# Attention scores from operands stacked on 128 partitions, and a new order of the mixer steps, in a two-layer hybrid encoder

## The chip, the cores and the metric

The kernel runs on one core of one Trainium2 chip. The metric is the device time of one execution in microseconds (us); lower is better. The profile is of one execution on that core.

## The reference, cut to what matters

The program is an encoder of two layers over 512 tokens of 1024 features, batch 1, float32 in and out. Each layer projects the normalised input once, sends the columns through three mixers, joins them, and ends with a two-matrix feed-forward part.

```python
for i in range(DEPTH):                                   # DEPTH = 2
    h = rmsnorm(x, norm_mix_g[i])
    p = h @ w_in[i]                                      # 1024 -> 2176 columns
    a_x, a_g, q, k, v, c_u = jnp.split(p, splits, axis=-1)
    y_a = rglru_mixer(a_x, a_g, ...)                     # gated linear recurrence, both directions
    y_b = window_attention(q, k, v, attn_sink[i], ...)   # 6 query heads, 2 key heads, |i-j| <= 128
    y_c = hyena_mixer(c_u, ...)                          # long convolution through a Fourier transform
    y = concatenate([rmsnorm(y_a), rmsnorm(y_b), rmsnorm(y_c)])
    x = x + y @ w_out[i]
    x = x + square(relu(rmsnorm(x) @ w_up[i])) @ w_down[i]
return rmsnorm(x, final_norm_g)

# inside window_attention, per block of 128 queries and its neighbouring blocks of keys
s = einsum("bnqhgd,bnshd->bnhgqs", qb, kb) * 64 ** -0.5  # the scores, contraction over 64
p = exp(s - m); denom = sum(p) + exp(sink - m)
o = einsum("bnhgqs,bnshd->bnqhgd", p / denom, vb)
```

## The kernel before, in words

**Precision.** TensorE multiplies in a rounded 32-bit format (float32r). To keep float32 accuracy, an operand is split into a rounded part hi and the remainder lo (`split`, L486), and a product is made of three: hi·hi, hi·lo, lo·hi (`mm3`, L501). Weights are split as they arrive (`split_weight`, L534): ScalarE or VectorE rounds, VectorE or GpSimd subtracts.

**Stages of a layer.** First 17 input tiles (`in_tile`, L876): each is 8 x 3 products of 512 columns into the PSUM tile `pin`, and VectorE takes it out. Tiles 0 to 5 belong to the recurrence (0-2 values, 3-5 gate), 6 to 8 are the queries (each tile has one head of key head 0 on partitions 0 to 63 and one of key head 1 on 64 to 127), 9 the keys, 10 the values, 11 to 16 the convolution. Then come the mixers, which overlap the input tiles as far as the order allows; then the output projection (`po`, L1168), then the feed-forward part (`up` L1186, `down` L1215: tiles `pu`, `pX`, `pY`, `pZ`). The filters of the convolution (`filters`, L757) are computed in layer 0's mixers for layer 0, and in layer 0's feed-forward part for layer 1.

**Attention** (`attention`, L992) is a generator of 8 units per layer: 4 query blocks times 2 key heads. A unit makes three score tiles `s`, one for each query head of the group. A score tile has 256 columns in the first and last query block and 384 in the two in the middle, so 24 tiles of either kind in the two layers. Each is three products with a contraction over 64 partitions (L1014 to L1016), then one or two bfloat16 mask products over 128 partitions (L1018, L1020). VectorE takes the row maximum `mx`, ScalarE the exponential `e` with its row sum, VectorE the reciprocal `es`; the rows are scaled, transposed on TensorE (`pt`), copied out (`pth`) and multiplied by the values (`pv`).

**The order.** `SCRIPTS` (L27) is an order of the steps of each layer, written out by hand: a number is an input tile, G0 to G2 the gates of the recurrence, S its scans, A its output gate, F the filters, I two further tables and the residual input, H the convolution, R the set-up of the attention (transposed values, and the queries and keys that `in_tile` has left in `proj`), U one attention unit, NA, NB, NC the three group norms. The script gives every operation its place in a list. A planner (`Plan.schedule`, L276) then runs through a simulated time with a cost for each operation (`Plan.cost`, L236), gives each engine the ready operation that stands first in the list, and writes down the order. On the chip each engine executes its instructions in exactly that written order. Among the costs is that of the recurrence's scan (`tensor_tensor_scan`, L943), for which the formula at L263 is used: 0.07 + 512 x 0.00104 = 0.60 us.

**Fillers.** Where the planner finds TensorE without work for a while, it writes small bfloat16 products of constant data into its order (`filler`, L1273; tile `wk`, 256 columns). They are ordinary instructions of the written order, and their number is fixed when the program is built. The planner also keeps account of TensorE's activity (L374 to L385) and counts a product over 64 rows or fewer as 0.55 of a full one.

**Buffers and queues.** SBUF tiles of 128x512 come from 69 slots (`sp`, L466); PSUM has 7 banks for all tiles (`ps`, L468) and one for the fillers. All DMAs go through SyncE's queue. Weights are fetched in the order of the input tiles in the script (`wseq`, L520), two tiles ahead (`LA`). DMAs of F, I and G wait in the plan until an input tile has begun (`plan.gate`).

Of the kernel before, what the change touches and what calls it, by code (L numbers as in the profile page):

```python
# [10 lines left out]
F32 = mybir.dt.float32  # L11
# [3 lines left out]
ALU = mybir.AluOpType  # L15
# [9 lines left out]
PRODUCTS = ["P1", "P2", "P6", "P5", "P7", "P3", "P4"]  # L25
OUT_PAIRS = [(6, 7), (0, 1), (2, 3), (4, 5)]
SCRIPTS = [q.split() for q in (  # L27
    "0 10 F 9 G0 2 8 3 1 11 G1 I G2 6 7 12 16 5 15 R U 4 S U 14 13 H U U A U NC U U U NA NB",
    "15 1 16 12 13 G1 8 2 11 6 G2 0 7 14 G0 H 9 10 R U 4 U 3 U U U NC 5 S A U U U NB NA",
)]  # L30
LA = 2
RESERVE = 7
# [134 lines left out]
class Plan:  # L167
# [67 lines left out]
    @staticmethod  # L235
    def cost(eng, name, args, kw, out):  # L236
        n = 1
        for d in out.shape[1:]:
            n *= d
        if name == "tensor_reduce":  # L240
            n = kw["in_"].shape[1]
        psum = any(isinstance(v, View) and v.base.pool.psum for v in list(args) + list(kw.values()))
        if name.startswith("dma"):
            return (out.shape[0] * n * 4 / 360e3, None)
        if eng == "tensor":
            if name == "transpose":
                return (n / 1200.0, None)
            dt = kw["lhsT"].base.dtype
            if dt == F32:
                return (4 * n / 2400.0, None)  # L250
            if dt == F32R and n < 256:
                return (4 * n / 2400.0, None)
            return (n / 2400.0 + (0.0133 if dt == F32R else 0.0025), None)
        if eng == "scalar":
            c = (0.051 if psum else 0.093) + n * 0.000833
            c += 0.093 * sum(isinstance(kw.get(k), View) for k in ("bias", "scale", "accum_out"))
            return (c, _TABLE.get(kw.get("func")))
        ptr = sum(isinstance(kw.get(k), View) for k in ("scalar1", "scalar2", "scalar"))
        if eng == "vector":
            if name == "reciprocal":  # L260
                return (0.06 + n * 0.00627, None)
            fast = name in ("tensor_scalar", "tensor_copy") and not psum
            return (0.07 + n * (0.00052 if fast else 0.00104) + 0.06 * ptr, None)  # L263
        if name in ("tensor_scalar", "memset"):
            return (0.13 + 0.06 * ptr + n * 0.00105, None)
        return (0.15 + n * 0.0021, None)
# [186 lines left out]
def encoder_kernel(ctx, tc, xT, w_in, w_out, w_up, w_down, gates, fw, par, trig, rope, decay, zemb, ident_d, maskb_d, yT):  # L453
    real_nc = tc.nc
    nc = plan = Plan()
# [15 lines left out]
    def R(name):  # L471
        return sp.tile([128, T], F32R, name=name, tag="s")
# [383 lines left out]
    for i in range(DEPTH):  # L856
# [9 lines left out]
        proj = {}  # L866
# [6 lines left out]
        def last_mark():  # L873
            return max(marks.values()) if marks else len(plan.ops) - 1

        def in_tile(m):  # L876
            p = PSM("pin")
            w = weight(("in", i, m))
            marks[m] = len(plan.ops)
            mm_tile(p, w, xs, kcs=in_kcs)  # L880
            if 6 <= m < 10:
                s, q = Fs("rs"), Fs("rq")
                plan.prio = EVP
                nc.vector.stream_shuffle(s, p, shuf)
                nc.vector.tensor_tensor(out=q, in0=p, in1=ropet[0], op=ALU.mult)
                plan.prio = 0.0
                nc.any.tensor_tensor(out=s, in0=s, in1=ropet[1], op=ALU.mult)
                nc.any.tensor_tensor(out=q, in0=q, in1=s, op=ALU.add)
                proj[m] = split(q, "k" if m == 9 else "q")
                return  # L890
            o = Fs("p%d" % m)
            plan.prio = EVP
            nc.vector.tensor_tensor(out=o, in0=p, in1=rstd, op=ALU.mult)
            plan.prio = 0.0
            proj[m] = o
# [94 lines left out]
            return vs  # L990

        def attention(qs, ks, vs, yb):  # L992
            kh, kl = ks
            plan.prio = ATTP
            for qb in range(4):
                k0, k1 = max(0, qb - 1), min(4, qb + 2)
                nk = k1 - k0
                qc = slice(qb * 128, qb * 128 + 128)
                po = None
                first = True  # L1000
                outp = PMX("pv")
                for g in range(2):
                    rows = slice(64 * g, 64 * g + 64)
                    mx = smallb.tile([128, 4], F32, name="mx", tag="sb")
                    rs = smallb.tile([128, 4], F32, name="rs", tag="sb")
                    mn = smallb.tile([128, 4], F32, name="mn", tag="sb")
                    mx.parts = rs.parts = True
                    ss, pes = [], []
                    for j in range(3):
                        s = PMX("s")  # L1010
                        kc = slice(k0 * 128, k1 * 128)
                        o = s[:, :nk * 128]
                        qh, ql = qs[j][0][rows, qc], qs[j][1][rows, qc]
                        nc.tensor.matmul(out=o, lhsT=qh, rhs=kh[rows, kc], start=True, stop=False)  # L1014
                        nc.tensor.matmul(out=o, lhsT=qh, rhs=kl[rows, kc], start=False, stop=False)
                        nc.tensor.matmul(out=o, lhsT=ql, rhs=kh[rows, kc], start=False, stop=False)  # L1016
                        if qb > 0:
                            nc.tensor.matmul(out=s[:, 0:128], lhsT=identb, rhs=maskb[:, 0:128], start=False, stop=(qb == 3))  # L1018
                        if qb < 3:
                            nc.tensor.matmul(out=s[:, (nk - 1) * 128:nk * 128], lhsT=identb, rhs=maskb[:, 128:256], start=False, stop=True)  # L1020
                        nc.vector.tensor_reduce(out=mx[:, j:j + 1], in_=o, op=ALU.max, axis=AX.X)
                        ss.append(o)
                    nc.vector.scalar_tensor_tensor(out=mn[:, 0:3], in0=mx[:, 0:3], scalar=-0.125, in1=nsink[:, i, 3 * g:3 * g + 3], op0=ALU.mult, op1=ALU.min)
                    for j in range(3):
                        e = Fs("e")
                        act(e[:, :nk * 128], ss[j], AF.Exp, scale=0.125, bias=mn[:, j:j + 1], accum_out=rs[:, j:j + 1])
                        pes.append(e)
                    sk = cols(i, "sink", 3 * g, 3 * g + 3)
                    es = smallb.tile([128, 4], F32, name="es", tag="sb")
                    nc.vector.tensor_tensor(out=es[:, 0:3], in0=mn[:, 0:3], in1=sk, op=ALU.add)  # L1030
                    act(es[:, 0:3], es[:, 0:3], AF.Exp)
                    nc.vector.tensor_tensor(out=es[:, 0:3], in0=rs[:, 0:3], in1=es[:, 0:3], op=ALU.add)
                    nc.vector.reciprocal(out=es[:, 0:3], in_=es[:, 0:3])
                    for j in range(3):
                        e = pes[j][:, :nk * 128]
                        plan.either(
                            ("any", "tensor_scalar", dict(out=e, in0=e, scalar1=es[:, j:j + 1], scalar2=1.0, op0=ALU.mult, op1=ALU.mult)),
                            ("scalar", "activation", dict(out=e, in_=e, func=AF.Copy, scale=es[:, j:j + 1])),
                        )
                    for kb in range(nk):  # L1040
                        pt = PMX("pt")
                        for j in range(3):
                            nc.tensor.transpose(pt[:, j * 128:j * 128 + 128], pes[j][:, kb * 128:kb * 128 + 128], ident)
                        th = Fs("pth")
                        plan.either(
                            ("scalar", "copy", dict(out=th[:, :384], in_=pt[:, :384])),
                            ("vector", "tensor_copy", dict(out=th[:, :384], in_=pt[:, :384])),
                        )
                        nc.tensor.matmul(out=outp[:, :384], lhsT=vs[g][:, k0 + kb, :], rhs=th[:, :384],
                                         start=(g == 0 and kb == 0), stop=(g == 1 and kb == nk - 1))  # L1050
                    if g == 1:
                        for j in range(3):
                            nc.scalar.copy(out=yb[j][:, qc], in_=outp[:, j * 128:j * 128 + 128])
                    plan.prio = 0.0
                    yield True
                    plan.prio = ATTP
            plan.prio = 0.0
# [69 lines left out]
        for step in SCRIPTS[i]:  # L1127
# [22 lines left out]
            elif step == "R":  # L1150
                ks = proj.pop(9)
                vs = v_tokens()
                qs = [proj.pop(6 + j) for j in range(3)]
# [266 lines left out]
```

## Time and profile before

| | us |
|---|---|
| median of 3 runs | 1166.24 (1161.07 to 1176.31) |
| the profiled execution, its own time | 1163.03 |
| its span, first to last instruction | 1161.2 |
| busy: TensorE (PE) / its weight loads (PEld) | 1143.8 / 920.2 |
| busy: VectorE (DVE) / ScalarE (ACT) / GpSimd (POOL) | 907.7 / 591.0 / 198.2 |

Times are in us from the first instruction. PE is TensorE's products, PEld its weight loads, which run beside them; products are pipelined, so the start of one to the start of the next (the pitch) tells what a product costs, and the shown duration of one is longer than that. PEclk is the clock that the chip granted TensorE, as a share of 2.4 GHz: it has the levels 2.4 and 1.2 GHz, so a mean of 0.9 in a stretch means a fifth of it at 1.2. All instructions carry line 449, where the planner issues them, so tiles are told apart by name. `a<-b,c` reads: tile a is written from b and c.

### The profile page before, as it was taken

What the parts mean: (1) busy time and instruction counts of PE and PEld (TensorE: products, weight loads), DVE (VectorE), ACT (ScalarE), POOL (GpSimd) and SP (SyncE); (2) the same over time, 40 slices, a digit from 0 to 9 for tenths busy, and PEclk for the clock granted to TensorE, in tenths of its full rate; (3) what the DMA queues carried; (4) which work ended last, traced back from release to release, by engine and by line L of the source; (5) the groups of instructions that cost most, each with busy time, mean ns of one, the idle gap of its engine ahead of it and who ended that gap; (6) DMA issues with size and microseconds to landing.
All of it is one profiled execution on the core that took longest, in us unless ns stands there. A gap on an engine that the chain in (4) does not pass through costs nothing.

```text
span 1161.2 us, 14314 instructions
## 1 busy us (share of the span) xinstructions
PE 1143.8 (98%) x5337; PEld 920.2 (79%) x5337; DVE 907.7 (78%) x1389; ACT 591.0 (51%) x956; POOL 198.2 (17%) x125
## 2 busy tenths in 40 slices
PE   9999899999999999999999999999999999999997
PEld 6778677888888788888888877678888888888886
DVE  8999786556797886886988989574587887797796
ACT  7564655455455354344465464572664454455344
POOL 0212221000110132100331142110010110111031
PEclk9999899999999999999999998899999999999999
DMA  9612100221422513422243211002213322431412
GB/s 351 246 52 91 41 15 1 84 81 54 137 98 80 171 38 108 127 77 87 90 155 109 89 55 56 1 19 91 91 38 126 127 78 86 146 107 57 127 55 73
DMA packets 35133, 107.92 MB, mean 93 GB/s; under 512 B 4150, under 2 KB 6710, under 8 KB 35064
## 3 DMA queue, kind: packets, MB, share of 16 engines
q1 hardware_dynamic: 35064, 107.01, 27.9%
q8 instruction: 42, 0.69, 0.2%
q14 instruction: 27, 0.22, 0.1%
HBM read 104.90 MB, written 2.10 MB: 92 GB/s over the span
## 4 chain that ended last, share of the span: by engine, by line
PE 90%; DVE 7%; ACT 2%; issue 1%; POOL 0%; DVEq 0%; POOLq 0%; ACTq 0%
PE pu L449 30%; PE pY L449 15%; PE pin L449 11%; PE pZ L449 8%; PE po L449 7%; PE pX L449 4%; PE s L449 3%; PE wk L449 3%; PE pv L449 3%; DVE tg L449 2%; PE pt L449 1%; PE f L449 1%; PE xt L449 1%; PE gate L449 1%; DVE wl L449 1%
## 5 line engine op out<-in xcount | busy, mean ns | idle before, releaser
L449 ACT CAST wh<-wr 128x1024 fp32r<-128x1024 f32 x189 | 199.4, 1056 | 356.9 <-PE pu L449 133.6
L449 DVE TENSOR_TENSOR wl<-wr,wh 128x1024 fp32r<-128x1024 f32 (+1 forms) x176 | 220.3, 1254 | 158.3 <-ACT wh L449 154.2
L449 PE MATMUL pu<-xgh,wl 128*128 128x512 f32 x512 | 199.4, 390 | 0.0
L449 PE MATMUL pu<-xgh,wh 128*128 128x512 f32 x512 | 199.4, 389 | 0.0
L449 PE MATMUL pu<-xgl,wh 128*128 128x512 f32 x512 | 199.3, 389 | 0.0
L449 POOL TENSOR_TENSOR wl<-wr,wh 128x1024 fp32r<-128x1024 f32 x51 | 123.1, 2416 | 257.0 <-ACT wh L449 153.5
L449 PEld LDWEIGHTS pu<-xgh,wl 128*128 128x128 f32 x512 | 96.1, 188 | 21.4 <-issue 1.6
L449 PEld LDWEIGHTS pu<-xgl,wh 128*128 128x128 f32 x512 | 96.1, 188 | 19.8
L449 PEld LDWEIGHTS pu<-xgh,wh 128*128 128x128 f32 x512 | 96.1, 188 | 19.7
L449 PE MATMUL pin<-xgh,wh 128*128 128x512 f32 x272 | 107.5, 395 | 0.4 <-ACT e L449 0.4
L449 PE MATMUL pin<-xgl,wh 128*128 128x512 f32 x272 | 107.5, 395 | 0.0
L449 PE MATMUL pin<-xgh,wl 128*128 128x512 f32 x272 | 107.5, 395 | 0.0
L449 POOL TENSOR_TENSOR s<-s,h 128x256 f32<-128x256 f32 x12 | 8.9, 740 | 397.7 <-ACT wh L449 388.8
L449 DVE TENSOR_TENSOR wr<-wr 128x1024 f32<-128x1024 f32 x61 | 72.9, 1219 | 0.0
L449 PEld LDWEIGHTS pin<-xgl,wh 128*128 128x128 f32 x272 | 51.4, 189 | 12.8 <-DVE xgl L449 1.8
L449 PEld LDWEIGHTS pin<-xgh,wh 128*128 128x128 f32 x272 | 51.3, 188 | 12.6 <-issue 1.1
L449 PEld LDWEIGHTS pin<-xgh,wl 128*128 128x128 f32 x272 | 51.2, 188 | 11.4 <-issue 0.8
L449 PE MATMUL po<-wh,ygh 128*128 128x512 f32 x128 | 50.8, 397 | 0.0
L449 PE MATMUL po<-wh,ygl 128*128 128x512 f32 x128 | 50.0, 396 | 0.0
L449 PE MATMUL po<-wl,ygh 128*128 128x512 f32 x128 | 50.0, 390 | 0.0
L449 DVE SCALAR_TENSOR_TENSOR x<-pY,r,x 128x512 f32<-128x512 f32 x64 | 45.6, 745 | 4.9 <-PE pY L449 4.9
L449 DVE SCALAR_TENSOR_TENSOR x<-pY,nr,x 128x512 f32<-128x512 f32 x64 | 45.8, 744 | 2.3 <-PE pY L449 2.3
(321 smaller groups left out, 2413.5 us busy)
## 6 DMA issues: line engine op xcount, KB each, us to landing
wr<-in_w_up SPq DMA_DIRECT2D x64, 512.0 KB, 3.5
wr<-in_w_down SPq DMA_DIRECT2D x64, 512.0 KB, 4.2
wr<-in_w_in SPq DMA_DIRECT2D x33, 512.0 KB, 5.7
wr<-in_w_out SPq DMA_DIRECT2D x16, 512.0 KB, 3.4
x<-in_xT SPq DMA_DIRECT2D x16, 256.0 KB, 4.6
dec<-in_decay SPq DMA_DIRECT2D x8, 256.0 KB, 6.8
out_y<-fin SPq DMA_DIRECT2D x16, 128.0 KB, 1.8
gt<-in_gates SPq DMA_DIRECT2D x6, 256.0 KB, 3.8
```

Of the source, the lines that this page charges most:

```text
L449: getattr(getattr(nc, o.eng), o.name)(*[res(a) for a in o.args], **{k: res(v) for k, v in o.kw.items()})
```

## The change

The three products of a score tile become two. `stack_query` makes, for each of the two heads of a query tile, one tile with the rounded query on its own 64 partitions and the remainder on the other 64. `stack_key` makes, for each key head, one tile with the rounded key on both halves and one with the key's remainder on both halves. A product of the stacked query with the first is hi·hi + lo·hi, with the second hi·lo + lo·lo, each over 128 partitions. The planner gets a cost for the scan of 0.06 + 512 x 0.00207 = 1.12 us. The two scripts have a new order of the same steps.

```diff
@@ -25,8 +25,8 @@
 PRODUCTS = ["P1", "P2", "P6", "P5", "P7", "P3", "P4"]
 OUT_PAIRS = [(6, 7), (0, 1), (2, 3), (4, 5)]
 SCRIPTS = [q.split() for q in (
-    "0 10 F 9 G0 2 8 3 1 11 G1 I G2 6 7 12 16 5 15 R U 4 S U 14 13 H U U A U NC U U U NA NB",
-    "15 1 16 12 13 G1 8 2 11 6 G2 0 7 14 G0 H 9 10 R U 4 U 3 U U U NC 5 S A U U U NB NA",
+    "8 10 F 9 0 G0 1 3 2 G1 12 G2 7 11 6 R 16 15 I 4 U 5 S 14 U 13 H U NC U U U U U A NA NB",
+    "1 16 12 13 G1 8 0 2 14 G2 15 6 G0 11 7 10 H 9 R U U U 4 S U U U 3 U 5 NC A U NB NA",
 )]
 LA = 2
 RESERVE = 7
@@ -260,6 +260,8 @@
             if name == "reciprocal":
                 return (0.06 + n * 0.00627, None)
             fast = name in ("tensor_scalar", "tensor_copy") and not psum
+            if name == "tensor_tensor_scan":
+                return (0.06 + n * 0.00207, None)
             return (0.07 + n * (0.00052 if fast else 0.00104) + 0.06 * ptr, None)
         if name in ("tensor_scalar", "memset"):
             return (0.13 + 0.06 * ptr + n * 0.00105, None)
@@ -873,6 +875,35 @@
         def last_mark():
             return max(marks.values()) if marks else len(plan.ops) - 1
 
+        halves = (slice(0, 64), slice(64, 128))
+
+        def rounded(out, src):
+            plan.either(("scalar", "copy", dict(out=out, in_=src)), ("vector", "tensor_copy", dict(out=out, in_=src)))
+
+        def stack_query(q):
+
+            out = []
+            for g in range(2):
+                a, b = halves[g], halves[1 - g]
+                t = R("qs")
+                rounded(t[a], q[a])
+                nc.vector.tensor_tensor(out=t[b], in0=q[a], in1=t[a].bitcast(F32), op=ALU.subtract)
+                out.append(t)
+            return out
+
+        def stack_key(k):
+
+            out = []
+            for g in range(2):
+                a, b = halves[g], halves[1 - g]
+                h, l = R("kh"), R("kl")
+                rounded(h[a], k[a])
+                rounded(h[b], k[a])
+                nc.vector.tensor_tensor(out=l[a], in0=k[a], in1=h[a].bitcast(F32), op=ALU.subtract)
+                rounded(l[b], l[a].bitcast(F32))
+                out.append((h, l))
+            return out
+
         def in_tile(m):
             p = PSM("pin")
             w = weight(("in", i, m))
@@ -886,7 +917,7 @@
                 plan.prio = 0.0
                 nc.any.tensor_tensor(out=s, in0=s, in1=ropet[1], op=ALU.mult)
                 nc.any.tensor_tensor(out=q, in0=q, in1=s, op=ALU.add)
-                proj[m] = split(q, "k" if m == 9 else "q")
+                proj[m] = stack_key(q) if m == 9 else stack_query(q)
                 return
             o = Fs("p%d" % m)
             plan.prio = EVP
@@ -990,7 +1021,6 @@
             return vs
 
         def attention(qs, ks, vs, yb):
-            kh, kl = ks
             plan.prio = ATTP
             for qb in range(4):
                 k0, k1 = max(0, qb - 1), min(4, qb + 2)
@@ -1000,7 +1030,6 @@
                 first = True
                 outp = PMX("pv")
                 for g in range(2):
-                    rows = slice(64 * g, 64 * g + 64)
                     mx = smallb.tile([128, 4], F32, name="mx", tag="sb")
                     rs = smallb.tile([128, 4], F32, name="rs", tag="sb")
                     mn = smallb.tile([128, 4], F32, name="mn", tag="sb")
@@ -1010,10 +1039,8 @@
                         s = PMX("s")
                         kc = slice(k0 * 128, k1 * 128)
                         o = s[:, :nk * 128]
-                        qh, ql = qs[j][0][rows, qc], qs[j][1][rows, qc]
-                        nc.tensor.matmul(out=o, lhsT=qh, rhs=kh[rows, kc], start=True, stop=False)
-                        nc.tensor.matmul(out=o, lhsT=qh, rhs=kl[rows, kc], start=False, stop=False)
-                        nc.tensor.matmul(out=o, lhsT=ql, rhs=kh[rows, kc], start=False, stop=False)
+                        nc.tensor.matmul(out=o, lhsT=qs[j][g][:, qc], rhs=ks[g][0][:, kc], start=True, stop=False)
+                        nc.tensor.matmul(out=o, lhsT=qs[j][g][:, qc], rhs=ks[g][1][:, kc], start=False, stop=False)
                         if qb > 0:
                             nc.tensor.matmul(out=s[:, 0:128], lhsT=identb, rhs=maskb[:, 0:128], start=False, stop=(qb == 3))
                         if qb < 3:
```

## Rows read from the trace of the kernel before

**Rows 1.** Page, part 1: busy us, share and instructions of each engine.
```profile
PE 1143.8 (98%) x5337; PEld 920.2 (79%) x5337; DVE 907.7 (78%) x1389; ACT 591.0 (51%) x956; POOL 198.2 (17%) x125
```
**Rows 2.** Windows: length, busy PE, PEld, DVE, ACT, POOL, PEclk, DMA share, GB/s.
```profile
300.00:325.00 25.00, 25.00 (x112) 20.71 (x111) 16.93 (x22) 9.41 (x12) 2.37 (x1) 1.00 0.44 133
...
0.00:140.00 140.00, 134.14 (x596) 102.00 (x596) 128.26 (x227) 85.36 (x134) 25.60 (x22) 0.98 0.46 161
140.00:207.00 67.00, 66.42 (x402) 50.52 (x402) 49.44 (x102) 37.70 (x95) 14.64 (x12) 0.97 0.03 9
...
715.00:772.00 57.00, 56.56 (x276) 36.82 (x277) 37.42 (x97) 38.51 (x101) 9.71 (x13) 0.88 0.03 10
```
**Rows 3.** Windows of the fillers alone (tile wk): length, busy PE, PEclk, DMA.
```profile
140.00:207.00 67.00, 12.47 (x93) 0.97 0.03 9
...
715.00:772.00 57.00, 9.52 (x64) 0.88 0.03 10
```
**Rows 4.** Chain that ended last, by line: 100 to 215, then 680 to 780.
```profile
by line: PE s L449 13.8%; PE pv L449 12.4%; PE pin L449 10.1%; DVE tg L449 9.0%; PE po L449 8.9%; PE wk L449 7.9%; PE pt L449 5.9%; PE y L449 5.0%; DVE p L449 4.1%; DVE cv L449 2.9%; PE Xo L449 2.5%; PE Xe L449 2.5%; PE ssq L449 2.3%; DVE w
...
by line: PE s L449 21.9%; PE pv L449 15.2%; PE po L449 7.8%; PE pt L449 7.0%; PE wk L449 6.5%; DVE t L449 5.6%; DVE tg L449 5.2%; issue 5.2%; DVE yc L449 4.0%; PE ssq L449 2.7%; DVE wl L449 2.3%; DVE G L449 1.9%; DVE Gl L449 1.9%; DVE X L44
```
**Rows 5.** Timeline of PE, a 256-column score tile: start, us, instruction.
```profile
116.84 0.39 PE L449 MATMUL pin<-xgh,wl 128*128 128x512 f32 x1
117.15 0.38 PE L449 MATMUL s<-kh,qh 64*128 64x256 f32 x1
117.38 0.28 PE L449 MATMUL s<-kl,qh 64*128 64x256 f32 x1
117.50 0.28 PE L449 MATMUL s<-kh,ql 64*128 64x256 f32 x1
117.70 0.23 PE L449 MATMUL s<-maskb,identb 128*128 128x128 bf16 x1
117.86 0.39 PE L449 MATMUL s<-kh,qh 64*128 64x256 f32 x1
```
**Rows 6.** Timeline of PE, a 384-column score tile and the next one's start.
```profile
140.06 0.44 PE L449 MATMUL s<-kh,qh 64*128 64x384 f32 x1
...
140.99 0.44 PE L449 MATMUL s<-kh,qh 64*128 64x384 f32 x1
```
**Rows 7.** Timeline of PE, products over 128 partitions with 256 columns.
```profile
176.26 0.28 PE L449 MATMUL y<-trigl,Gh 128*128 128x256 f32 x1
176.38 0.28 PE L449 MATMUL y<-trigh,Gl 128*128 128x256 f32 x1
```
**Rows 8.** Tile qh: min/median/max ns of the queries' rounding and subtraction.
```profile
L449 DVE TENSOR_TENSOR ql<-rq,qh x6: 673/682/693, 52.2 to 666.9; 128x512 fp32r<-128x512 f32 x6
L449 DVE CAST qh<-rq x4: 409/412/429, 51.2 to 652.4; 128x512 fp32r<-128x512 f32 x4
L449 ACT CAST qh<-rq x2: 623/624/626, 100.5 to 666.3; 128x512 fp32r<-128x512 f32 x2
```
**Rows 9.** Window of DVE alone: length, busy us, PEclk, DMA share, GB/s.
```profile
25.00:125.00 100.00, 96.85 (x150) 0.98 0.37 129
```
**Rows 10.** Timeline of DVE in layer 1: the keys' first and last step.
```profile
688.95 0.67 DVE L449 TENSOR_TENSOR rq<-pin,ropet 128x512 f32<-128x512 f32 x1
...
709.84 0.68 DVE L449 TENSOR_TENSOR rq<-rq,rs 128x512 f32<-128x512 f32 x1
```
**Rows 11.** Groups by shape: the scan (count, busy us, mean ns).
```profile
L449 DVE TENSOR_TENSOR_SCAN tg<-a,tg 128x512 f32<-128x512 f32 x12 | 17.4, 1481 | 0.0
```
**Rows 12.** Timeline of PE: a stall in layer 0 (idle before, releaser).
```profile
123.13 1.54 PE L449 MATMUL pt<-ident,e 128*128 128x128 f32 x6 [2.85 <-POOL e L449]
```
**Rows 13.** Timelines around 170: fillers, what follows them, ACT's last rounding before it.
```profile
168.36 7.94 PE L449 MATMUL wk<-warmc 128*128 128x256 bf16 x56
176.06 0.36 PE L449 MATMUL y<-trigh,Gh 128*128 128x256 f32 x1
...
170.36 0.62 ACT L449 CAST Gh<-G 128x512 fp32r<-128x512 f32 x1 [1.79 <-DVE es L449]
```

## Prediction

> **What bounds the kernel now.** I read the page's busy times first: TensorE is busy for 98% of the span, VectorE for 78%, ScalarE for 51% [rows 1]. So I then cut the span into stages. In the feed-forward part TensorE starts 112 products of 512 columns in 25 us, 0.22 us each, at full clock and without a gap [rows 2]: nothing there changes. The two ends of the mixers, 140 to 207 in layer 0 and 715 to 772 in layer 1, look just as full (66.4 of 67 and 56.6 of 57 us busy), but 12.5 and 9.5 us of that are fillers [rows 3], and the granted clock is 0.97 and 0.88 [rows 2], so part of the stretch ran at 1.2 GHz. In these ends the input tiles are used up and TensorE has only the attention and the convolution.
>
> The chain of waits says what sets their length. In the 115 us from 100 the score tiles hold 13.8% of the chain, in the 100 us from 680 they hold 21.9%, more than any other tile [rows 4]: 15.9 + 21.9 = 37.8 us. The 48 score tiles cost about 39 us in all (below), so nearly all of their time is on the chain. Fillers are on it too (7.9% and 6.5%). That is the point of a written order: a filler is executed even if TensorE is late, so time lost against the plan isn't made up by leaving fillers out.
>
> **The score products.** A 256-column score tile takes 0.71 us, from 117.15 to 117.86 [rows 5]. The second of its products costs 0.12; the first lasts 0.23 until the next, the third 0.20, the mask product 0.16. The step from the 128-row product of the input tile to the first 64-row one is 0.31, where 512 columns cost 0.22. A 128-row product of 256 columns costs 0.12 as well [rows 7], so the number of rows itself costs nothing; it is the change between 64 and 128 rows, twice in each tile, that costs some 0.3 us. With two products of 128 rows the tile should take 2 x 0.12 and 0.06 for the mask (half of 256 columns; no row shows a mask without the change): 0.30, so 0.41 less. A 384-column tile takes 0.93, 140.06 to 140.99 [rows 6]; one product lies between 0.12 for 256 and 0.22 for 512, so 0.17, and the tile becomes 2 x 0.17 + 2 x 0.06 = 0.46, so 0.47 less. For 24 tiles of each kind: 24 x (0.41 + 0.47) = 21.1 us. Of that 7.0 us, 24 x (0.12 + 0.17), is the third product and 14.1 the changes of rows, a cost that no formula of the planner holds.
>
> How much reaches the end? At least nothing, if the row maxima and exponentials behind the scores set the pace at once; at most all 21.1. The chain shows 37.8 of 39 us of score time on it, which is near the upper end; but a faster score tile of 0.46 us comes close to what VectorE needs for its maximum, so that is late next. I take 85%: 17.9 us.
>
> The Trainium skill has a rule against this change: TensorE: Matmul & The Clock Gate, in the section on packing small matmuls, says that products over few rows run at the same time if they sit in different row groups, so two 64-row products could share the array and 128-row ones can't. By that rule three 64-row products would cost as much as one and a half full ones, and the change would add half a product per tile, 24 x 0.5 x (0.12 + 0.17) = 3.5 us by our rows. Rows 5 don't bear it out: the kernel before issues the three products of one head in a row, all on the same half, and each takes its full 0.12.
>
> **The added vector work.** Before, a layer had 4 roundings and 4 subtractions for three query tiles and the keys. After, each query tile has 2 and 2, the keys 6 and 2: 12 and 8. Both layers add 16 roundings and 8 subtractions. Half the partitions save nothing that I can count on, so I take the full tile's times: a rounding is 0.41 us on VectorE or 0.62 on ScalarE, a subtraction 0.68 [rows 8]. All on VectorE that is 16 x 0.41 + 8 x 0.68 = 12.0 us, 6 per layer; the other bound is nothing, if it all lies in gaps, and a gain is excluded since nothing is taken away. From 25 to 125 VectorE is busy for 96.9 of 100 us [rows 9], just where layer 0 makes these operands, so about 3 of its 6 us find room and 3 don't; the ends are emptier (49.4 of 67, 37.4 of 57) [rows 2], so I add 1 for layer 1. Cost: 4 us.
>
> The keys of layer 1 are worse placed: their tile is the last before R in both scripts, and in the old one their first vector step at 688.95 is followed by the last one only at 709.84 [rows 10], because VectorE has the convolution's work ahead of it. The first score waits for that. Before, a rounding came next; now two roundings, the subtraction and one more rounding stand in sequence for the second product: at 0.62 and 0.68 that is 1.2 to 2 us more for one head, and 5.1 for both (6 x 0.62 + 2 x 0.68) if they go one behind another, against nothing if input tiles cover it. I take 2 us.
>
> **The new order and the scan's cost.** What can be won: the stall at 123 (2.85 us, transposes ahead of input products waited for a scaled exponential) [rows 12]; the clock, where a mean of 0.98 over 140 us loses 2.8 us of work, 0.97 over 67 us 2.0 and 0.88 over 57 us 6.8 [rows 2]; and fillers past their use: 56 of them run from 168.36 to 176.06, while ScalarE's last rounding for the next products ended at 170.98, 5.1 us earlier [rows 13]. Together 19.6 us. They come from VectorE and TensorE being later than planned. The scan takes 1.48 us on average [rows 11]; the plan counts 0.60 and will count 1.12, so 0.52 of the 0.88 us that it misses, 59%, becomes known, and the changes of rows go altogether. Against that, any new order may have stalls of its own. Bounds: all 19.6 won, or 10 lost (two stalls like that at 123, with as much again in clock after each). I take about half: 9.5 us won.
>
> Of the moved steps, I has ten DMAs of 256 KB and moves in layer 0 from behind eight input tiles to behind thirteen. What it loads is first read after 176 (tables of y) and by the output projection; the DMA engines are at 3% from 140 to 207 [rows 2], so it costs nothing unless those 40 us of slack were used up. F stays third, and the number of weight fetches is the same. Tile 8 comes first instead of 0; both wait for the same norm of x. A moves behind the last U of layer 0; its three activations and three products, some 3.9 us at the 0.62 and 0.68 of tiles of that size [rows 8], can go into ScalarE's gaps beforehand or beside the first output products, which use group C. I count nothing, and 4 us in the range.
>
> **Sum.** The profiled execution took 1163.0 us, 1.8 more than its span and 3.2 below the median of the three runs. 1163.0 - 17.9 - 9.5 + 4 + 2 = 1141.6, so 1142 us: 1.8% below the profiled execution, 2.1% below the median.
>
> **The rivals.**
>
> *The saved time returns as waiting.* VectorE's maxima, ScalarE's exponentials and the 7 PSUM banks set the pace of the ends, and fillers fill what TensorE saves. For it: fillers are there already [rows 3]. Against: the scores lead the chain [rows 4]. Then a third of the 21.1 arrives, 7, the order gives 4 and the additions cost 6: 1158 us. Chance 0.22.
>
> *Everything falls into place.* All 21.1 us and nearly all of the 19.6 arrive, say 18, with 4 of additions: 1128 us. For it: both come from one cause, a plan that didn't know how late the engines were. Against: the order of before was also written by a planner. Chance 0.18.
>
> *The change of rows stays.* If the 0.3 us belonged to the change of data type at the bfloat16 mask, the masks would keep it, and only the third product goes: 7.0 x 0.85 = 6. Then 1163.0 - 6 - 8 + 6 = 1155. Against it: the step from input tile to score costs 0.09 extra though both are float32r [rows 5]. Chance 0.06. [...]
>
> *VectorE becomes the bound, and it gets slower.* It has 3.1 us free between 25 and 125 [rows 9]. If ScalarE takes no roundings, 12.0 us are added; once a layer's 6 exceed what is free, every score starts later by the rest, the score time is no longer on the path (saved: 0), and when the input tiles run out TensorE waits and drops to 1.2 GHz in layer 0 as it does in layer 1 (6.8 us lost there). 1163.0 + 12.0 + 6.8 = 1182. Chance 0.06.
>
> **How the numbers follow.** The forecast has the remaining 0.48, with 1133 to 1151 as its own range. To hold 8 in 10 the range takes in the case of everything on one side and most of the case of returned waiting on the other: 1121 to 1162. Two per cent is about what a measurement of this kernel can tell from no change; from 1163 the border lies at 1140. Below it fall the case of everything (0.18) and half of the forecast (0.24): 0.42. Slower by over 2%, above 1186, is a part of the last rival: 0.03. Within: 0.55.
>
> **What would show it.** Right: score tiles of two 128-row products at a pitch of 0.30 and 0.46 us with no longer first product; 48 fewer score products; their share of the chain down by half; a clock above 0.95 in layer 1's end; ends of the mixers 8 to 14 us shorter each. The feed-forward stage must be unchanged. Wrong: more filler time than 22 us in the ends (first rival); a mask product still 0.16 to 0.20 behind the scores (third); idle TensorE before the first score of a layer, released by the keys' tiles, with VectorE full (last).

## The result, and the profile after

The changed kernel takes 1130.9 us (median of 4 runs, 1128.3 to 1134.8) against 1166.0 for the kernel before: a ratio of 0.969, with a 95% interval of 0.962 to 0.976. That is 3.1% less time: faster than the 1142 us that I forecast, and inside the range of 1121 to 1162. The profiled execution took 1134.8 us, the longest of the four; that of the kernel before took 1163.0.

First the stages of both profiles, as windows cut where a stage begins: layer 0's mixers until the first `pu`, its feed-forward part, layer 1's mixers (from the first `xt`), the rest. Columns: length, busy TensorE with its products, PEclk, DMA share, GB/s. Before:

```profile
0.00:246.80 246.80, 240.35 (x1186) 0.98 0.31 109
246.80:591.20 344.40, 344.40 (x1549) 1.00 0.31 100
591.20:819.12 227.92, 223.76 (x1090) 0.97 0.20 66
819.12:1161.20 342.08, 335.25 (x1518) 1.00 0.28 93
```

After:

```profile
0.00:234.20 234.20, 228.52 (x1128) 0.98 0.34 115
234.20:578.50 344.30, 344.30 (x1549) 1.00 0.31 100
578.50:791.75 213.25, 208.19 (x1047) 0.99 0.22 71
791.75:1133.00 341.25, 335.27 (x1518) 1.00 0.29 93
```

Of the 28.2 us between the two spans, 12.6 are from layer 0's mixers and 14.7 from layer 1's; the feed-forward parts are the same to a microsecond. The gain is where the change is.

The timeline of TensorE after, two score tiles of 256 columns behind each other, and one of 384 up to the next one's first product:

```profile
114.65 0.28 PE L451 MATMUL s<-kh,qs 128*128 128x256 f32 x1
114.76 0.28 PE L451 MATMUL s<-kl,qs 128*128 128x256 f32 x1
114.89 0.23 PE L451 MATMUL s<-maskb,identb 128*128 128x128 bf16 x1
114.92 0.36 PE L451 MATMUL s<-kh,qs 128*128 128x256 f32 x1
115.12 0.28 PE L451 MATMUL s<-kl,qs 128*128 128x256 f32 x1
115.25 0.23 PE L451 MATMUL s<-maskb,identb 128*128 128x128 bf16 x1
115.28 0.36 PE L451 MATMUL s<-kh,qs 128*128 128x256 f32 x1
...
137.31 0.42 PE L451 MATMUL s<-kh,qs 128*128 128x384 f32 x1
137.56 0.34 PE L451 MATMUL s<-kl,qs 128*128 128x384 f32 x1
137.75 0.29 PE L451 MATMUL s<-maskb,identb 128*128 128x128 bf16 x2
137.84 0.42 PE L451 MATMUL s<-kh,qs 128*128 128x384 f32 x1
```

A tile takes 0.36 us (114.92 to 115.28) and 0.53 (137.31 to 137.84), where [rows 5] and [rows 6] had 0.71 and 0.93. The mask follows the last product after 0.13 us, no longer 0.20. What I missed: a first product that stands behind a bfloat16 mask takes 0.20 us until the next, one that stands behind a float32r product 0.11 (the first line). So a small part of what I put down to the rows was the mask's. The rows had it: behind the bfloat16 fillers of [rows 13] the first `y` product starts at 176.06 and, in [rows 7], the second at 176.26.

Who waits for the scores has changed. The groups by shape for VectorE's row maximum (count, busy us, mean ns, then idle time before them and its releaser), before:

```profile
L449 DVE TENSOR_REDUCE mx<-s 128x1 f32<-128x384 f32 x24 | 13.3, 556 | 13.5 <-PE s L449 13.5
```

and after:

```profile
L451 DVE TENSOR_REDUCE mx<-s 128x1 f32<-128x384 f32 x24 | 12.5, 546 | 1.2 <-PE s L451 1.2
```

VectorE stood still for 13.5 us for these tiles and now for 1.2: at a pitch of 0.53 us, the scores come as fast as VectorE takes their maxima (546 ns each). The chain of waits after, by line, 100 to 200 and 650 to 760, answers to [rows 4]:

```profile
by line: PE po L451 12.9%; PE pv L451 10.6%; DVE wl L451 7.4%; DVE cv L451 6.9%; PE pt L451 6.4%; PE wk L451 6.4%; PE s L451 6.3%; PE y L451 5.7%; DVE tg L451 5.5%; issue 4.9%; DVE p L451 3.7%; PE Xe L451 3.4%; PE Xo L451 3.1%; PE ssq L451 
...
by line: PE po L451 13.8%; PE pv L451 9.0%; DVE tg L451 6.5%; PE s L451 6.3%; issue 5.6%; DVE t L451 5.5%; DVE wl L451 5.4%; PE pt L451 4.5%; ACT e L451 3.7%; DVE mx L451 2.4%; PE Xo L451 2.3%; ACT L451 2.3%; DVE X L451 2.3%; DVE yc L451 2.
```

The scores fell from 13.8% and 21.9% to 6.3% in both, and VectorE's own work has come up the list.

### The profile page after: what moved, and what is told of

It is laid out like the page before. It is cut to its first block, busy times and chain, and to the rows that moved or that the text cites. A ratio compares the mean times of both kernels' runs of the same rounds, so it can differ in the third digit from the quotient of the medians.

```text
span 1133.0 us, 14123 instructions
## 1 busy us (share of the span) xinstructions
PE 1116.3 (99%) x5234; PEld 904.9 (80%) x5234; DVE 916.6 (81%) x1401; ACT 593.3 (52%) x967; POOL 196.4 (17%) x123
## 4 chain that ended last, share of the span: by engine, by line
PE 86%; DVE 10%; ACT 2%; issue 1%; DMA 0%; SPq 0%; DVEq 0%; ACTq 0%
PE pu L451 31%; PE pY L451 15%; PE pin L451 8%; PE po L451 8%; PE pZ L451 8%; PE pX L451 4%; DVE wl L451 2%; PE pv L451 2%; PE wk L451 2%; DVE tg L451 1%; PE gate L451 1%; PE f L451 1%; PE s L451 1%; PE pt L451 1%; PE xt L451 1%
## 5 line engine op out<-in xcount | busy, mean ns | idle before, releaser
L451 DVE TENSOR_TENSOR wl<-wr,wh 128x1024 fp32r<-128x1024 f32 (+1 forms) x179 | 225.3, 1261 | 156.2 <-ACT wh L451 152.0
L451 POOL TENSOR_TENSOR wl<-wr,wh 128x1024 fp32r<-128x1024 f32 x48 | 115.3, 2405 | 237.9 <-ACT wh L451 126.2
L451 PEld LDWEIGHTS pin<-xgh,wh 128*128 128x128 f32 x272 | 51.1, 188 | 10.9 <-ACT wh L451 0.4
```

The lines of the kernel that those rows point to most:

```text
L451: getattr(getattr(nc, o.eng), o.name)(*[res(a) for a in o.args], **{k: res(v) for k, v in o.kw.items()})
```

## The experiments

### Which part of the change it was

The change has three parts, and five more kernels take it apart; of the eight combinations only the new cost alone was not run. The stacked operands alone (the diff's `stack_query`, `stack_key` and the two products):

```diff
-                proj[m] = split(q, "k" if m == 9 else "q")
+                proj[m] = stack_key(q) if m == 9 else stack_query(q)
```

> Stacked operands alone, with the old order of steps and the old cost of the scan. Theory P (the score products carry the gain): the tiles of scores save 24 x (0.35 + 0.40) = 18 us and most of it arrives, less 6 us of vector work, so 1163 - 12 to - 18, 1145 to 1151, and clock and fillers at the ends of the mixers are better than before. Rival O (the new order carries the gain): saved product time turns into fillers and waits, 1155 to 1165.

The new `SCRIPTS` alone, in the kernel before:

> New order of steps alone, three 64-row products as before and the old cost of the scan. Theory P: the order is worth 0 to 10 us, so 1153 to 1163. Rival O: 15 to 25 us, 1138 to 1148. It may also be slower than before, since the order was written for cheaper scores.

The whole change without the new `SCRIPTS`:

> The whole change but the old order of steps. Theory P: 1138 to 1148 (the products' 12 to 18 us, and some us from a plan that knows the scan's time). Rival O: 1150 to 1160. The difference to the changed kernel (1131) is what the new order is worth on top.

The whole change without the new cost:

```diff
-            if name == "tensor_tensor_scan":
-                return (0.06 + n * 0.00207, None)
```

> The whole change but the old cost of the scan in the planner. My prediction had 59% of VectorE's lag behind the plan removed by the new cost: if so 3 to 6 us slower than the changed kernel, 1134 to 1137, with stalls of TensorE for VectorE after the scans. If the scan's cost is nothing but a reason to write another order: within 2 us of 1131, either way.

And the new `SCRIPTS` and the new cost with the old score products:

> New order and new cost of the scan, but the three 64-row products as before: what the stacked operands are worth within the new order. The 128-row form at a fixed order was worth 20 us and the third product 1.5; the vector work of stacking costs something. Theory D (the changes of rows and the clock they take along): 12 to 20 us slower than the changed kernel, 1143 to 1151, with tiles at 0.71 and 0.93 us. Rival (the new order hides the products): within 5 us of 1131.

The ratios are to the kernel before as it ran in the same sitting, so they compare better than the medians: its own median was 1166.0 us for the first and last line, 1168.6 for the last but one and 1168.9 for the others.

| stacked operands | new order | scan cost | us, median | ratio to before (95% interval) | fillers |
|---|---|---|---|---|---|
| no | no | 0.60 | 1166.0 | 1 | 289 |
| yes | no | 0.60 | 1158.4 | 0.991 (0.988 to 0.993) | 445 |
| no | yes | 0.60 | 1147.9 | 0.982 (0.977 to 0.988) | 201 |
| yes | no | 1.12 | 1159.7 | 0.991 (0.988 to 0.994) | 466 |
| yes | yes | 0.60 | 1145.0 | 0.980 (0.973 to 0.986) | 293 |
| no | yes | 1.12 | 1155.1 | 0.987 (0.981 to 0.993) | 278 |
| yes | yes | 1.12 | 1130.9 | 0.969 (0.962 to 0.976) | 234 |

Three kernels came out as the rival expected: stacking alone (1158.4), the order alone (1147.9) and all but the order (1159.7). But the new order does not carry the gain by itself: without the new cost it takes 1145.0 us, in neither of the ranges expected there, and without stacking it is 24 us slower than the changed kernel, more than the 12 to 20 expected. The parts don't add up. By the medians stacking alone gives 7.6 us, order and cost without it 10.9, and all together 35.1. By the ratios stacking is worth 0.9% at the old order, 0.2% at the new one with the old cost (0.982 to 0.980, not to be told from nothing), and 1.8% at the new one with the new cost (0.987 to 0.969). The new cost does nothing at the old order with stacking (0.991 twice), makes the new one no faster without stacking (0.982 to 0.987, within the intervals), and is worth 1.1% where all three are together. A part changes not only its own instructions but the planner's whole written order.

The last column points to a reading. Among the four orders with stacking the times stand in the order of their fillers: 234, 293, 445, 466 for 1130.9, 1145.0, 1158.4, 1159.7 us. The three orders without stacking stand in that order too: 201, 278, 289 for 1147.9, 1155.1, 1166.0. With the old order the planner meets the cheaper scores with 156 more fillers. By the traces the fillers keep TensorE busy for 56.6 us there, against 40.7 before: 15.9 us came back as planned waiting, my first rival. Its sign was more than 22 us of fillers in the ends of the mixers. It is there with stacking alone, 32.0 us (windows of the fillers alone: length, busy, PEclk, DMA share, GB/s):

```profile
140.00:250.00 110.00, 15.83 (x139) 1.00 0.14 47
700.00:830.00 130.00, 16.12 (x137) 1.00 0.17 53
```

and not in the changed kernel, 13.3 us:

```profile
140.00:250.00 110.00, 7.65 (x58) 1.00 0.16 53
700.00:830.00 130.00, 5.63 (x44) 1.00 0.18 57
```

That this waiting is what the old order costs is argued from the counts; no run takes the added fillers of stacking alone away.

### The score products at an unchanged order

To price the products without a new plan, the next two kernels let the planner write the order of before and edit instructions only as they are issued: TensorE's sequence otherwise stays the same. Products over all 128 partitions, still three:

```diff
         for o in order:
+            if o.eng == "tensor" and o.name == "matmul" and o.kw["out"].base.name == "s" and o.kw["lhsT"].shape[0] == 64:
+                for q in ("lhsT", "rhs"):
+                    v = o.kw[q]
+                    o.kw[q] = v.base[:, v.ops[-1][1][1]]
```

> The kernel before with its written order kept to the last instruction, but each of the three score products reads all 128 partitions of the query and key tiles instead of 64 (this leaves the scores wrong: both heads of a tile are summed). Only the changes between 64 and 128 rows go. Theory D (they cost TensorE time that nothing hides): tiles at a pitch of about 0.5 and 0.7 us instead of 0.71 and 0.93, 10 us less in TensorE's time and 6 to 10 us less in the total, with the same 289 fillers. Rival (the time was cover for VectorE and ScalarE): 0 to 3 us less, and TensorE's idle time goes up by the rest.

and the third product dropped as well:

```diff
+            if o.eng == "tensor" and o.name == "matmul" and o.kw["out"].base.name == "s" and o.kw["lhsT"].base.name == "ql":
+                continue
```

> The same, and the third score product (query remainder times key) is left out when the order is issued: the written order otherwise unchanged. Theory D: a further 5 to 7 us less than with three 128-row products. Rival: no difference beyond 1 to 2 us. Added to the former, the difference to the kernel before is what cheaper scores are worth at the old order, without the added vector work; stacking alone gave 10 us with that work.

Measured: 1146.4 us, ratio 0.980 (0.975 to 0.984), and 1144.9, ratio 0.979 (0.974 to 0.983). So 128 rows instead of 64, with the same number of products, are worth 20 us by the medians, all by themselves, twice the 6 to 10 that I expected. The third product is worth 1.5: clear of nothing, since no execution of one kernel overlaps with one of the other, but as little as the rival expected. The timeline of the first shows a tile of 256 columns with three products:

```profile
110.22 0.36 PE L453 MATMUL s<-kh,qh 128*128 128x256 f32 x1
110.42 0.28 PE L453 MATMUL s<-kl,qh 128*128 128x256 f32 x1
110.53 0.28 PE L453 MATMUL s<-kh,ql 128*128 128x256 f32 x1
110.65 0.23 PE L453 MATMUL s<-maskb,identb 128*128 128x128 bf16 x1
110.69 0.36 PE L453 MATMUL s<-kh,qh 128*128 128x256 f32 x1
```

0.47 us where the kernel before had 0.71, from the number of rows alone. The tile with 384 columns took 0.71 instead of 0.93 in the same way. For 24 tiles each that is 24 x (0.24 + 0.22) = 11 us of pitch, an estimate, since some tiles are interleaved with other products. The rest is in the clock. The two profiled executions differ by 16.9 us of span (1161.2 and 1144.3). Their mean granted clock over the span is 0.989 and 0.994, so 0.011 x 1161.2 = 12.8 and 0.006 x 1144.3 = 6.9 us were lost at 1.2 GHz: 5.9 us less, and with the 11 of pitch 16.9. Windows of 700 to 780, the end of layer 1's mixers, before:

```profile
700.00:780.00 80.00, 77.94 (x390) 0.91 0.07 21
```

the same order with 128 rows:

```profile
700.00:780.00 80.00, 77.46 (x440) 1.00 0.10 34
```

and the new order with the three 64-row products:

```profile
700.00:780.00 80.00, 80.00 (x389) 0.91 0.08 26
```

A mean of 0.91 is 18% of 80 us at 1.2 GHz, 7.2 us lost. All kernels whose scores are 128-row products show 1.00 here with their fillers in place; those with 64-row ones show 0.91, 0.96 and 0.91. The window flatters the edited order a little, though. Just ahead of it, from 680 to 700, before and then with 128 rows:

```profile
680.00:700.00 20.00, 17.91 (x104) 1.00 0.11 36
680.00:700.00 20.00, 17.89 (x85) 0.91 0.16 53
```

And the clock of one kernel differs between executions. The kernel before had means from 0.976 (1174.9 us) to 0.994 (1158.7 us); the edited order had 0.994 or 0.995 in all four executions. At an equal 0.994 the two are 12.5 us apart (1158.7 and 1146.2), close to the 11 of pitch. So more than half of the 20 us is the products' own time and the rest the clock. Whether the 64-row products lower the clock themselves or by the waits that come with them, no run separates; the new order with 64-row products reached 0.995 in one execution.

The Trainium skill (TensorEngine Tiling (Array Packing), Key Properties) says that a change of tiling mode drains TensorE; the pitches agree, some 0.23 us per tile for two changes.

### Fillers past their use

Fillers left out as the order is issued, in the kernel before and in the changed one:

```diff
         for o in order:
+            if o.idx < 0:
+                continue
```

> The kernel before with all 289 fillers left out when the order is issued, all else in the same order. If fillers run past their use, 3 to 10 us less. If they only fill time in which TensorE waits, no less, and if they hold the clock up, more: the granted clock at the ends of the mixers falls below 0.88 and the time rises by 5 to 20 us.

> The changed kernel with its fillers left out in the same way. If its fillers hold the clock up: its clock at the ends, 1.00 in the profile, falls to that of the kernel before (0.9) and the time rises by 5 to 20 us. If they are only idle time: within 3 us of 1131.

Before: 1172.2 us, ratio 1.004 (1.000 to 1.007), 6 us slower by the medians. The clock of its windows shows why nothing is won (the first is layer 0's end, the second layer 1's):

```profile
140.00:207.00 67.00, 59.22 (x278) 0.77 0.03 9
...
715.00:772.00 57.00, 51.81 (x218) 0.76 0.04 14
```

Against 0.97 and 0.88 in [rows 2]. What TensorE saves by leaving fillers out it loses at 1.2 GHz. The changed kernel without fillers takes 1135.7 us, ratio 0.971 (0.966 to 0.977), 4.8 us slower by the medians and within the intervals, between the two expectations; its clock in 700 to 757 falls from 1.00 to 0.94. So in these two orders the fillers stand in waiting that the order holds; they aren't the cause of it.

### Is it the scan's true time, or these very numbers?

The planner's scan cost set to the mean of the trace before, 1.48 us:

```diff
-                return (0.06 + n * 0.00207, None)
+                return (0.06 + n * 0.00277, None)
```

> The changed kernel with the planner's scan cost raised from 1.12 to 1.48 us, the mean that the trace shows. Theory S (a plan that knows VectorE's lag wins): 1126 to 1132, no slower than the changed kernel. Theory F (the new scripts fit exactly the plan they were written with, and any other number gives another order and loses): 1135 to 1150.

And two small moves, a table load at 1.28 instead of 1.30 (L387), and VectorE's latency at 0.16 instead of 0.15 (L159):

> The changed kernel with one planner number moved by next to nothing: a load of ScalarE's tables counts 1.28 us (as the trace shows) instead of 1.30. Theory S: within 2 us of 1131. Theory F: another written order, 1135 to 1147, as far off as leaving out the scan's cost was (1145).

> The changed kernel with VectorE's latency in the planner 0.16 instead of 0.15 us. Theory S: within 2 us of 1131. Theory F: 1135 to 1147.

Measured: 1146.4 us, ratio 0.980 (0.974 to 0.985) with the cost of 1.48; 1133.4, 0.969 (0.962 to 0.976) and 1134.6, 0.969 (0.963 to 0.975) with the small moves. The first of these doesn't test what it was meant to test. The 1.48 us is a mean of twelve scans that a few long ones raise. Their durations (count, min/median/max ns, first and last start) in the kernel before and in the kernel planned with 1.48:

```profile
L449 DVE TENSOR_TENSOR_SCAN tg<-a,tg x12: 1192/1213/3349, 98.7 to 723.8; 128x512 f32<-128x512 f32 x12
L451 DVE TENSOR_TENSOR_SCAN tg<-a,tg x12: 1199/1216/1223, 103.1 to 715.4; 128x512 f32<-128x512 f32 x12
```

The usual scan takes 1.21 us. So the change's 1.12 is the cost nearest to the trace; 0.60 is 0.61 too low and 1.48 is 0.27 too high, and both are 14 to 16 us slower (1145.0 and 1146.4). That fits theory S. It doesn't show it, since at the old order the nearer cost gave nothing. Theory F expected the small moves to lose as well, and they don't. But they hardly gave another order: TensorE's sequence of products, by tile names, differs from the changed kernel's in 2 lines of 5234 with the first and 81 with the second, against 460 with 1.48. Whether the result depends on these very sequences stays open. The order of the fillers holds again, but not their size: 400 fillers come with 1146.4 us, where 293 came with 1145.0. Tile `wk` in these three kernels, in that order (count, duration min/median/max, first and last start):

```profile
L451 PE MATMUL wk<-warmc x400: 272/273/421, 1.2 to 1135.0; 128*128 128x256 bf16 x134
```
```profile
L451 PE MATMUL wk<-warmc x234: 272/273/422, 1.2 to 1121.1; 128*128 128x256 bf16 x117
```
```profile
L451 PE MATMUL wk<-warmc x233: 272/273/422, 1.2 to 1125.4; 128*128 128x256 bf16 x117
```

With 400 fillers the planner foresaw 166 more slots of waiting than with 234. Whether scripts written for another cost would do as well as these do at 1.12 wasn't tried.

## Why the prediction was right, and where its terms were off

**What the result confirms.** The direction was right, and the time lies in the range. But the range of 1121 to 1162 takes in all six changed kernels of the table, so that says little about the mechanism; the terms have to be looked at one by one.

**The score products: right in size, wrong in make-up.** I took 17.9 us of 21.1: 14.1 for the changes of rows and 7.0 for the third product. At an unchanged order the two together gave 21 us (1166.1 to 1144.9). But the changes of rows alone gave 20 and the third product 1.5. By pitch the rows give 11 us; I had not charged them with the clock, half of which I counted as a gain of the new order. The third product's pitch was right (0.47 to 0.36 us and 0.71 to 0.53, 7.0 us), but TensorE's busy time fell by only 4.9 us (1124.2 to 1119.3), and its idle time rose by 3.5 of them. With three 128-row products VectorE's maxima of 384 columns waited for scores only 2.1 us in all, instead of 13.5, so scores faster still would have waited for VectorE; that this is the whole reason wasn't tested. By pitch the tiles save 24 x (0.35 + 0.40) = 18.0 us, not 21.1: the first product behind a mask takes 0.20 where I took 0.12.

**The rival in which the change of rows stays** is excluded as a whole: with the masks kept and 128 rows the tile falls from 0.71 to 0.47. A piece of it is true: a first product behind a mask costs 0.20 us, with 128 rows too. That two 64-row products on different halves could share the array is not tested by any run: the kernel before issues the three products of one head in a row, and of those in [rows 5] only the second takes 0.12 us.

**The added vector work: the place was right.** In the written order that won, 18 of the 24 roundings went to ScalarE and all 16 subtractions to VectorE, in tiles of 64x512 that mostly take what full ones do (a subtraction 687 ns at the median, with one of 1677):

```profile
L451 DVE TENSOR_TENSOR qs<-rq,qs x12: 685/687/1677, 41.7 to 668.4; 64x512 fp32r<-64x512 f32 x12
L451 ACT CAST qs<-rq x9: 617/619/622, 40.7 to 665.8; 64x512 fp32r<-64x512 f32 x9
```

VectorE did not become the bound: from 25 to 125 it is busy for 93.1 us against 96.9 in [rows 9], the last rival's ground. The wait that I expected at layer 1's first scores is there, in the timeline of TensorE:

```profile
701.30 0.98 PE L451 MATMUL s<-kh,qs 128*128 128x256 f32 x6 [0.88 <-ACT kh L451]
...
704.90 0.39 PE L451 MATMUL s<-kl,qs 128*128 128x256 f32 x1 [0.56 <-ACT kl L451]
```

0.88 + 0.56 = 1.4 us behind the keys' roundings, for the 2 that I took. At the old order, with stacking alone, the work costs more: in layer 0 TensorE stands still before two scores until VectorE is done,

```profile
114.99 0.39 PE L449 MATMUL s<-kh,qs 128*128 128x256 f32 x1 [2.87 <-DVE qs L449]
118.45 0.58 PE L449 MATMUL s<-kh,qs 128*128 128x256 f32 x1 [2.78 <-DVE p L449]
```

5.7 us, of which the first half is the stacked query's subtraction. What the vector work costs in all no run shows by itself; the 13.5 us between stacking at the old order and the edited order with two products (1158.4 and 1144.9) also hold the planner's 156 more fillers.

**The new order and the scan: the term that was missing.** I took half of 19.6 us, 9.5, and added the terms as if each kept its size beside the others. Without stacking, order and cost gave 10.9 us (1166.0 to 1155.1), close to the 9.5. On top of stacking they gave 27.5 (1158.4 to 1130.9). The parts alone make 18.5 us of the 35.1; the other 16.6 come only when all are together, and my sum put that at nothing. The 11 us that my forecast misses are less than this. My reading is that the order acts on the same waiting into which the cheaper products turn at the old order; it rests on the filler counts and isn't shown by itself.

My reason for the 9.5, that 59% of VectorE's unforeseen lag becomes known, had the wrong share: by the usual scan of 1.21 us it is 0.52 of 0.61, 85%. And knowing it isn't enough: at the old order, with stacking, the same cost gives nothing. "Fillers past their use" as 5.1 us to be won found no support: without fillers the kernel before is no faster, but its clock falls too, so this doesn't price the 5.1 by themselves.

**The chances.** The result lies between the case of "everything falls into place", 1128 us with 0.18, and the forecast's own 1133 to 1151. The reason of that case, a plan that didn't know how late the engines are, isn't shown. Returned waiting, 1158 us with 0.22, is what stacking alone came to, 1158.4.

## What to carry to other kernels

Where products of 64 and 128 rows alternate in a written order, price the change itself: here it was 0.23 us of pitch per tile, 11 us, and a lower clock beside it, 20 us in all, more than leaving out a third of the products. If a planner writes the order, price an edit with the order frozen and with a new one: two 128-row products gave 21 us in the frozen order and 8 to 11 in the one that the planner wrote for them (which holds the added vector work too). Then try a new order for the cheaper work. The number of fillers ranked the orders here, but did not say by how much they differ. And before a cost is taken from a trace, look at its median beside the mean.

## What the runs showed that I had not expected

In one profiled execution each, the granted clock over 80 us stood at 0.91 with three 64-row products per tile and at 1.00 with three 128-row ones, in the same order with the same 289 fillers. A float32r product behind a bfloat16 mask took 0.20 us until the next where one behind a float32r product took 0.11, both with 128 rows and 256 columns. A third fewer score products moved the total by 1.5 us only. A few long scans among twelve, one of 3.35 us, made a mean of 1.48 out of a usual 1.21.
